# An encoder layer on one core: the Mamba-2 branch turned round, written in an order by hand for four engines, with weight fetches moved ahead

## The chip, the cores and the metric

The kernel runs on one core of a Trainium2 chip. The metric is the device time of one execution in microseconds (us). Five engines work beside each other: PE (TensorE, matmuls; its weight loads are shown as PEld), DVE (VectorE), ACT (ScalarE), POOL (GpSimd) and SP (SyncE, which here only issues DMAs). Each takes its instructions in a fixed order; where one waits, all behind it on that engine wait.

## The reference, cut to what matters

One layer: x is normalised and projected by one matrix `w_in` to the columns of three branches (Mamba-2, RWKV-7, HGRN2) and of three merge gates; each branch runs a scan forward and one backward and sums them; the branches are projected, gated, merged, and a feed-forward block follows. 1024 tokens, width 1024. The part that the change rewrites is the Mamba-2 branch (16 heads of 64, 2 groups of 8 heads, state 128, chunks of 128 tokens):

```python
xbc = jax.nn.silu(centred_depthwise_conv(xbc, conv_w, conv_b))
...
dt = jax.nn.softplus(dt_raw.reshape(b, L, 2, SSM_HEADS) + dt_bias)
y_f = ssd_chunked(xs, dt[:, :, 0], a[0], bm, cm)
y_b = flip_t(ssd_chunked(flip_t(xs), flip_t(dt[:, :, 1]), a[1], flip_t(bm), flip_t(cm)))
y = y_f + y_b + xs * d_skip[:, None]
y = y.reshape(b, L, SSM_INNER) * jax.nn.silu(z)
return rmsnorm(y, norm_w)
```

`ssd_chunked` computes in each chunk of 128 tokens: a part within the chunk (the products C·B, each times an exponential of differences of cumulated `dt*a`, applied to x), the chunk's own addition to the state (B times weighted x), and a part from the state that the chunk receives (C times that state, times an exponential).

## The kernel before

**The filler.** The input projection is cut into 79 jobs of 16 steps (`Jobs`, 1264 steps). A step is three matmuls of 128x512 (lines L330 to L332, `mm`): weights split in two parts `wh` and `wl`, x split likewise. The steps are handed out as filler between the pieces of the branches: `J.share(w)` emits a number of steps in proportion to `w` out of the table `FILL`, `J.get(...)` those that a branch needs first. Each job's 512 KB of raw weights come by a DMA that ACT issues (`wr`, L219), ACT casts them to `wh` (L221), DVE (or POOL) forms `wl` (L223). Results go from PSUM through `st` (L272) to DRAM (`pg` for the gates).

**The order.** A scheduler places instructions on each engine from the program's order, priorities and its own estimates of time, so that filler may be moved ahead of pieces that wait. Within `manual_schedule(engines=...)` the named engines keep the order in which the code is written.

**The Mamba-2 branch** (`ssd`, behind RWKV and HGRN2): a setup (`dt`, cumulated sums, their rows stored to DRAM as `cumd`), then for each of two groups: six convolutions (`conv`: tile `pt` from DRAM by SP, one ACT pass L1297, four DVE passes L1299, a Silu L1301), two for B and C and four for x; C·B products `cbps` (L1324), transposes `btps` (L1325) and `xps` (L1346, copied by ACT to `xt`); then the loop over i = 0..7, which I call the core: the forward chunk i and the backward chunk 7-i are treated in the same turn. `pairs` (L1362) makes the exponentials of a chunk for 8 heads: rows of `cumd` are broadcast by DMA into `E` (128x1024) for each direction, POOL subtracts (L1369), DVE picks one direction by a mask (L1372), ACT takes the exponential (L1373), DVE multiplies by C·B (L1374). PE computes `yo` (L1390, C times the state `S`), `st` (L1398, the chunk's addition to the state) and `yd` (L1409, eight products with `E`); DVE weights x (`xw`, L1396) and forms `yt` (L1392); POOL decays `S` (L1402) and adds to `Y` (L1393, L1383). `yo` and `st` share two PSUM buffers (tag `b`). In the region from L1378 only POOL's order is written by hand. After the core `Y` is transposed (`ytps`, L1429), multiplied by Silu(z) (`zs`) and stored.

## Time and profile before

| | before |
|---|---|
| median of 3 runs | 2424.53 us (2424.19 to 2427.28) |
| profiled execution | 2423.01 us, of which the trace spans 2421.3 us |
| mean granted TensorE clock | 0.973 |
| PE busy | 2272.7 us (94%) |
| DVE, POOL, ACT busy | 65%, 43%, 41% |
| first `st` of the core | at 1135.24 us of the span |

The span runs from the first instruction to the last. Busy shares overlap, since engines work beside each other; what an engine's idle time cost is read from its waits. Matmuls are pipelined: the durations of single matmuls overlap, so the time of one is read from the distance of two starts. An f32 matmul (`st`, `yo`, `yd`, the transposes) has two records each; an `mm` has one.

### The profile page before, as it was taken

The numbers are of one execution on the slowest core, as the hardware profiler recorded it, in microseconds if no ns is written. First come the engines' busy times: TensorE is split into PE (matmuls) and PEld (weight loads), VectorE is DVE, ScalarE is ACT, GpSimd is POOL, SyncE is SP. The second block draws the span as 40 slices with busy tenths as digits, with TensorE's granted clock in tenths as the row PEclk, the third lists the DMA queues.
The fourth block names the chain that finished last, engine by engine and source line by source line (L and its number), as shares of the span: only waits on it lengthen the run. The fifth ranks groups of instructions, "written<-read, shape, count | busy, mean of one in ns | idle before, by whom it ended". The sixth has DMA issues, their size and how long they took to land.

```text
span 2421.3 us, 37438 instructions
## 1 busy us (share of the span) xinstructions
PE 2272.7 (94%) x14785; PEld 1838.1 (76%) x14785; DVE 1570.6 (65%) x2041; ACT 988.7 (41%) x1436; POOL 1040.8 (43%) x817
## 2 busy tenths in 40 slices
PE   8998999999998998998999889999899999999895
PEld 6776778788777877887678567888688888877674
DVE  5678764455558568545856776442764554479999
ACT  6554532222466655435134154332433333344333
POOL 4433331543134335202941841430454444457985
PEclk9999999999999999999999999999999999999998
DMA  5455784764442232245545555541232222244211
GB/s 151 122 139 136 176 212 112 225 199 124 142 150 98 82 118 79 75 160 146 135 156 142 129 191 193 168 130 61 66 101 87 79 87 79 98 163 131 95 54 70
DMA packets 381212, 306.23 MB, mean 126 GB/s; under 512 B 111273, under 2 KB 323149, under 8 KB 381037
## 3 DMA queue, kind: packets, MB, share of 16 engines
q1 hardware_dynamic: 260909, 225.71, 31.7%
q10 hardware_dynamic: 119936, 77.61, 11.1%
q8 instruction: 116, 1.90, 0.3%
q0 software_dynamic: 192, 0.52, 0.1%
q14 instruction: 59, 0.48, 0.1%
HBM read 209.68 MB, written 94.11 MB: 125 GB/s over the span
## 4 chain that ended last, share of the span: by engine, by line
PE 61%; DVE 20%; POOL 5%; DMA 5%; issue 4%; ACT 4%; SPq 1%; ACTq 0%; DVEq 0%; POOLq 0%
PE mm L330 7%; PE mm L331 7%; PE mm L332 7%; PE ps L1588 6%; PE ps L1589 6%; PE ps L1590 6%; DVE ab L1805 3%; DVE acc L1927 2%; PE mm L231 2%; PE mm L232 2%; PE mm L233 2%; DMA E<-cumd 2%; POOL E L1369 2%; DVE rb L1805 1%; PE mm L1588 1%
## 5 line engine op out<-in xcount | busy, mean ns | idle before, releaser
L330 PE MATMUL mm<-x,wh 128*128 128x512 f32 (+1 forms) x1232 | 500.3, 406 | 0.6 <-ACT wh L221 0.5
L331 PE MATMUL mm<-x,wh 128*128 128x512 f32 (+1 forms) x1232 | 492.6, 400 | 0.0
L332 PE MATMUL mm<-x,wl 128*128 128x512 f32 (+1 forms) x1232 | 489.9, 398 | 0.0
L330 PEld LDWEIGHTS mm<-x,wh 128*128 128x128 f32 (+1 forms) x1232 | 232.8, 189 | 62.0 <-issue 10.3
L332 PEld LDWEIGHTS mm<-x,wl 128*128 128x128 f32 (+1 forms) x1232 | 232.8, 189 | 54.2 <-issue 4.6
L331 PEld LDWEIGHTS mm<-x,wh 128*128 128x128 f32 (+1 forms) x1232 | 232.8, 189 | 53.7 <-issue 7.0
L1589 PE MATMUL ps<-xb,rb 128*128 128x512 f32 x432 | 168.3, 390 | 0.0
L1590 PE MATMUL ps<-xb,rb 128*128 128x512 f32 x432 | 168.3, 390 | 0.0
L1588 PE MATMUL ps<-xb,rb 128*128 128x512 f32 x432 | 168.3, 390 | 0.0
L221 ACT CAST wh<-wr 128x1024 fp32r<-128x1024 f32 (+2 forms) x103 | 100.2, 973 | 109.4 <-PE mm L331 87.4
L1588 PE MATMUL ps<-rb,ab 128*128 128x512 f32 x308 | 125.9, 409 | 18.3 <-DVE acc L1927 17.4
L223 POOL TENSOR_TENSOR wl<-wr,wh 128x1024 fp32r<-128x1024 f32 x30 | 79.2, 2640 | 133.9 <-ACT wh L221 109.9
L1589 PE MATMUL ps<-rb,ab 128*128 128x512 f32 x308 | 123.7, 402 | 2.9 <-POOL rb L1805 2.9
L223 DVE TENSOR_TENSOR wl<-wr,wh 128x1024 fp32r<-128x1024 f32 (+2 forms) x73 | 95.2, 1303 | 44.9 <-ACT wh L221 44.8
L1590 PE MATMUL ps<-rb,ab 128*128 128x512 f32 x308 | 122.4, 400 | 1.5 <-DVE ab L1805 1.5
L1752 ACT CAST rb<-fs 128x512 fp32r<-128x512 f32 x85 | 52.6, 622 | 167.2 <-PE ps L1590 117.7
L272 ACT COPY st<-mm 128x512 f32<-128x512 f32 x130 | 75.3, 580 | 99.1 <-PE mm L332 82.9
L1369 POOL TENSOR_TENSOR E<-E,cums 128x1024 f32<-128x1024 f32 x32 | 69.3, 2178 | 65.5 <-DMA E<-cumd 45.3
L810 DVE TENSOR_TENSOR Gc<-Gps,mk 128x256 f32<-128x256 f32 x64 | 27.2, 425 | 106.0 <-PE Gps L807 59.9
L231 PE MATMUL mm<-oh,wh 128*128 128x512 f32 x224 | 89.5, 403 | 6.5 <-DVE gt L1492 4.3
L1927 DVE TENSOR_TENSOR acc<-acc,ps 128x512 f32<-128x512 f32 x148 | 94.1, 674 | 0.0
L1589 PEld LDWEIGHTS ps<-xb,rb 128*128 128x128 f32 x432 | 81.1, 188 | 16.9
(504 smaller groups left out, 5397.2 us busy)
## 6 DMA issues: line engine op xcount, KB each, us to landing
wr<-in_w_in_dram ACTq DMA_DIRECT2D x74, 512.0 KB
fr<-in_ffn_w_in_dram SPq DMA_DIRECT2D x44, 512.0 KB
E<-cumd SPq DMA_DIRECT2D x32, 512.0 KB
pg<-st ACTq DMA_DIRECT2D x48, 256.0 KB
gt<-pg SPq DMA_DIRECT2D x24, 512.0 KB
ad<-a SPq DMA_DIRECT2D x22, 512.0 KB
dr<-in_ffn_w_down_dram SPq DMA_DIRECT2D x22, 512.0 KB
ar<-ad SPq DMA_DIRECT2D x22, 512.0 KB
```

The costliest lines, as they stand in the source:

```text
L221: nc.scalar.copy(hi[:, :kt, :n], raw[:, :kt, :n])
L223: g.lo_eng.tensor_sub(lo[:, :kt, :n], raw[:, :kt, :n], f32(hi[:, :kt, :n]))
L231: nc.tensor.matmul(ps, whi[:, k, :n], xh, start=(k == 0), stop=False)
L330: g.nc.tensor.matmul(ps[:n], w[0][:, k, :n], xh, start=(k == 0), stop=False)
L331: g.nc.tensor.matmul(ps[:n], w[0][:, k, :n], xl, start=False, stop=False)
L332: g.nc.tensor.matmul(ps[:n], w[1][:, k, :n], xh, start=False, stop=(k == KT - 1))
L1369: nc.gpsimd.tensor_tensor(e, e, cs.unsqueeze(2).broadcast_to([P, 8, P]), SUB)
L1588: nc.tensor.matmul(ps, ah, bh, start=(i == 0), stop=False)
L1589: nc.tensor.matmul(ps, ah, bl, start=False, stop=False)
L1590: nc.tensor.matmul(ps, al, bh, start=False, stop=(i == n - 1))
L1805: eng.tensor_sub(blk[:, 1], s, f32(blk[:, 0]))
L1927: nc.vector.tensor_add(m[j], m[j], ps)
```

## The change

Three things, all inside one diff:

1. `Jobs` fetches the raw weights of job i+2 when the second half of job i begins (`fetch`), where before those of job i+1 were loaded when job i began.
2. The core is turned round. All seven states of the backward direction are formed first and kept (`Sb`), then one pass over the chunks i = 0..7 forms y of both directions, already transposed (channels on partitions): `yo` becomes four matmuls with a piece of the state as weights and `CT` as the moving side, for each direction, `yd` has `xt` (64 columns) as weights and `E` as the moving side and writes to alternating halves of the 128 partitions. The exponential of the row that `yo` is multiplied with (`X`) comes from the `E` tile by ACT. The transposes `ytps` after the core are gone. Silu(z) is computed before the core, stored to DRAM (`zd`) and read back chunk by chunk (`z`); the output goes out chunk by chunk. Of POOL's work, the decay of S goes to DVE, half of the subtractions to ACT (eight passes of 128x128 a chunk), the additions to `Y` fall away; a small one remains. DVE gets a second masked copy (`id8`), which sets the diagonal. `st` has PSUM tag `b` for itself; `yo` and `yd` share tag `a`.
3. The region written by hand now holds PE, ACT, DVE and POOL, and `FILL["ss"]` is a new table.

```diff
-    "ss": (4, 36, 12, 18, 6, 3, 8, 5, 22, 13, 8),
+    "ss": (4, 30, 12, 5, 5, 12, 22, 8, 5, 18),
...
+def load_raw(g, src, kt, n=P, tag="w"):
     raw = g.wpool.tile([P, KT, P], F32, tag=tag + "r", name=tag + "r", bufs=g.wraw_bufs)
     g.wq.dma_start(raw[:, :kt, :n], src.rearrange("(k p) c -> p k c", p=P))
+    return raw
+def load_w(g, src, kt, n=P, tag="w", raw=None):
+    nc = g.nc
+    if raw is None:
+        raw = load_raw(g, src, kt, n, tag)
...
+    def source(self, i):
+        job = self.jobs[i]
+        return self.g.A["w_in"][0][:, job.c0:job.c0 + job.n], KT, job.n
+    def fetch(self, i):
+        if 4 <= i < len(self.jobs) and i not in self.raws:
+            self.g.wq = self.g.nc.scalar
+            self.raws[i] = load_raw(self.g, *self.source(i))
...
+        return load_w(g, *self.source(i), raw=self.raws.pop(i, None))
...
         for half in range(2):
+            if half == 1:
+                self.fetch(i + 2)
...
-            nc.vector.tensor_sub(cums, cums, ld)
+            nc.vector.tensor_sub(cums, ld, cums)
...
+        m8, id8 = (kp.tile([P, P], U8, tag=n, name=n) for n in ("m8", "id8"))
         nc.vector.tensor_copy(m8, mlt)
+        nc.vector.tensor_copy(id8, g.ident)
...
-                J.share(F[1] + F[9] * grp)
+                J.share(F[1] + F[7] * grp)
...
+                nc.vector.tensor_add(gd, dtT[:, :, grp * 8:grp * 8 + 8], dtT[:, :, 16 + grp * 8:24 + grp * 8])
+                nc.vector.tensor_tensor(gd, gd, cbd.unsqueeze(2).broadcast_to([P, NT, 8]), MUL)
...
+                for q in range(grp * 4, grp * 4 + 4):
+                    zs = sp.tile([P, L + 4], F32, tag="E", name="zs", bufs=EB)[:, :L]
+                    nc.sync.dma_start(zs, J.get(g.pz, q))
+                    nc.scalar.activation(zs, zs, AF.Silu)
+                    nc.sync.dma_start(zd[q], zs)
...
+                def rows(c):
                     Es = []
                     for d in range(2):
                         e = sp.tile([P, L + 4], F32, tag="E", name="E", bufs=EB)
                         e = e[:, :L].rearrange("p (h t) -> p h t", t=P)
+                        h0 = d * 16 + grp * 8
+                        nc.sync.dma_start(e, cumd[h0:h0 + 8, c * P:(c + 1) * P].unsqueeze(0).broadcast_to([P, 8, P]))
                         Es.append(e)
+                    return Es
+                def exponents(c, Es):
+                    Xs = []
+                    for d in (1, 0):
+                        e, h0 = Es[d], d * 16 + grp * 8
+                        X = yp.tile([P, 4, P], F32, tag=f"X{d}", name="X", bufs=2)
+                        if c != (0, NT - 1)[d]:
+                            for b in range(2):
+                                hr = slice(b * 64, b * 64 + 64)
+                                nc.scalar.activation(X[hr], e[hr, b::2], AF.Exp)
+                        cs = cums[:, c, h0:h0 + 8]
+                        if d == 0:
+                            for h in range(8):
+                                nc.scalar.activation(e[:, h], e[:, h], AF.Identity, bias=cs[:, h:h + 1])
+                        else:
+                            nc.gpsimd.tensor_tensor(e, e, cs.unsqueeze(2).broadcast_to([P, 8, P]), ADD)
+                        Xs.insert(0, X)
+                    return Xs
+                def pick(Es):
+                    nc.vector.copy_predicated(Es[0], m8.unsqueeze(1).broadcast_to([P, 8, P]), Es[1])
+                def decays(c, e):
+                    nc.scalar.activation(e, e, AF.Exp)
+                    yield
+                    nc.vector.tensor_mul(e, e, CB[:, c:c + 1, :].broadcast_to([P, 8, P]))
+                    nc.vector.copy_predicated(e, id8.unsqueeze(1).broadcast_to([P, 8, P]),
+                                              gd[:, c].unsqueeze(2).broadcast_to([P, 8, P]))
+                    yield
+                def gate(c):
+                    z = yp.tile([P, 4, P], F32, tag="z", name="z", bufs=2)
+                    nc.sync.dma_start(z, zd[grp * 4:grp * 4 + 4, :, c * P:(c + 1) * P].rearrange("q p t -> p q t"))
+                    return z
...
+                Sb = yp.tile([P, NT - 1, 512], F32, tag="Sb", name="Sb")
+                Sa = yp.tile([P, 512], F32, tag="Sa", name="Sa")
+                def weighted(d, c):
+                    xw = yp.tile([P, 512], F32, tag="xw", name="xw", bufs=2)
+                    nc.vector.tensor_tensor(h3(xw), h3(xt[:, c]), per_head(wst, c, d), MUL)
+                    return xw
+                def update(d, c, xw, old, new):
+                    ps = pp.tile([P, 512], F32, tag="b", name="st", bufs=2)
+                    nc.tensor.matmul(ps, Bt[:, c], xw, start=True, stop=True)
+                    if old is None:
+                        nc.vector.tensor_copy(new, ps)
+                    else:
+                        nc.vector.tensor_tensor(h3(new), h3(old), per_head(dec, c, d), MUL)
+                        nc.vector.tensor_add(new, new, ps)
...
+                order = ExitStack()
+                order.enter_context(tc.manual_schedule(engines={PE, ACT, DVE, POOL}))
+                Es = rows(0)
+                X, z = exponents(0, Es), gate(0)
+                ahead = rows(1)
+                xw = weighted(1, NT - 1)
+                pick(Es)
+                for _ in decays(0, Es[0]):
+                    pass
+                J.share(F[9])
+                for c in range(NT - 1, 0, -1):
+                    xn = weighted(1, c - 1) if c > 1 else weighted(0, 0)
+                    update(1, c, xw, Sb[:, c] if c < NT - 1 else None, Sb[:, c - 1])
+                    xw = xn
+                    J.share(F[3])
+                for i in range(NT):
+                    ts = slice(i * P, (i + 1) * P)
+                    nEs = ahead
+                    if i + 2 < NT:
+                        ahead = rows(i + 2)
+                    if i + 1 < NT:
+                        nX, nz = exponents(i + 1, nEs), gate(i + 1)
+                    part = []
+                    for d, S in ((1, Sb[:, i] if i < NT - 1 else None), (0, Sa if i else None)):
+                        if S is None:
+                            continue
+                        ps = pp.tile([P, 4, P], F32, tag="a", name="yo", bufs=3)
+                        for q in range(4):
+                            nc.tensor.matmul(ps[:, q], S[:, q * P:(q + 1) * P], CT[:, ts], start=True, stop=True)
+                        nc.vector.tensor_mul(X[d], X[d], ps)
+                        part.append(X[d])
+                    if i < NT - 1:
+                        update(0, i, xw, Sa if i else None, Sa)
+                    J.share(F[4])
                     e = Es[0]
+                    ps = pp.tile([P, 4, P], F32, tag="a", name="yd", bufs=3)
                     for h in range(8):
+                        nc.tensor.matmul(ps[h % 2 * 64:h % 2 * 64 + 64, h // 2], xt[:, i, h * 64:h * 64 + 64], e[:, h],
                                          start=True, stop=True)
+                    y = part[0]
+                    if len(part) > 1:
+                        nc.vector.tensor_add(y, y, part[1])
+                    nc.vector.tensor_add(y, y, ps)
+                    nc.vector.tensor_mul(z, z, y)
+                    nc.sync.dma_start(ysc[grp * 4:grp * 4 + 4, :, ts].rearrange("q p t -> p q t"), z)
+                    nc.scalar.activation(y, z, AF.Square)
+                    nxt = iter(())
+                    if i + 1 < NT:
+                        pick(nEs)
+                        nxt = decays(i + 1, nEs[0])
+                        next(nxt)
+                    if i + 2 < NT:
+                        xw = weighted(0, i + 1)
+                    eng = nc.vector if grp and i == NT - 1 else nc.gpsimd
+                    eng.tensor_add(y[:, 0:2], y[:, 0:2], y[:, 2:4])
+                    if grp == 0:
+                        eng.tensor_add(ss[:, ts], y[:, 0], y[:, 1])
+                    else:
+                        eng.tensor_add(y[:, 0], y[:, 0], y[:, 1])
+                        eng.tensor_add(ss[:, ts], ss[:, ts], y[:, 0])
+                    next(nxt, None)
                     J.share(F[5])
+                    if i + 1 < NT:
+                        Es, X, z = nEs, nX, nz
```

What becomes of the order is seen at three places; the lines of the new code are about 20 higher in the parts before the core (L350 to L352 are the three matmuls of a filler step that were L330 to L332).

**PE, the setup of the first group, up to the first `st`.** Before (`btps` and `xps` are transposes of the setup, `mm` is filler):

```order
L332 MATMUL mm<-x_436,wl 128x512
L330 MATMUL mm<-x_190,wh 128x512
L1325 MATMUL btps<-ident,BT 128x128 x4
L1346 MATMUL xps<-ident,xq 128x128 x8
L331 MATMUL mm<-x_191,wh 128x512
L332 MATMUL mm<-x_190,wl 128x512
L330 MATMUL mm<-x_199,wh 128x512
L331 MATMUL mm<-x_200,wh 128x512
L332 MATMUL mm<-x_199,wl 128x512
L330 MATMUL mm<-x_208,wh 128x512
```

and now, at the corresponding place (the rows end with the first filler after the first `st`):

```order
L1345 MATMUL btps<-ident,BT 128x128
L1344 MATMUL cbps<-CT,BT 128x128
L1345 MATMUL btps<-ident,BT 128x128
L1344 MATMUL cbps<-CT,BT 128x128 x4
L1345 MATMUL btps<-ident,BT 128x128 x4
L1366 MATMUL xps<-ident,xq 128x128 x32
L1440 MATMUL st<-xw,Bt 128x512
L350 MATMUL mm<-x_199,wh 128x512
L351 MATMUL mm<-x_200,wh 128x512
```

Up to the end of the last but one run of `vps` matmuls (a product of HGRN2's last head) the filler is the same in both. Before, 12 steps follow and then the last 16 `vps`, and 127 more stand between these and the first `st`, so that 1026 of the 1264 steps are ahead of the first `st`. Now some 10 steps follow, then the last 16 `vps`, and no step stands between these and the first `st` (897 ahead of it); four stand between the first and the second `st`, and likewise behind each of the next. The filler that was among the end of HGRN2 and the setup has moved behind the first `st`.

**DVE, the start of the core.** Before:

```order
L223 TENSOR_TENSOR wl<-wr,wh 128x1024
L1396 TENSOR_TENSOR xw<-xt,wst 128x512
L1372 COPY_PREDICATED E<-m_10178,E 128x1024
L1396 TENSOR_TENSOR xw<-xt,wst 128x512
L1374 TENSOR_TENSOR E<-E,CB 128x1024
L223 TENSOR_TENSOR wl<-wr,wh 128x1024
L1372 COPY_PREDICATED E<-m_10178,E 128x1024
L1400 COPY S_10620<-st 128x512
L1396 TENSOR_TENSOR xw<-xt,wst 128x512
```

and now:

```order
L1319 SCALAR_TENSOR_TENSOR acc<-pt,vcolsv_443,acc 128x1024 x8
L1435 TENSOR_TENSOR xw<-xt,wst 128x512
L1413 COPY_PREDICATED E<-m_10174,E 128x1024
L1419 TENSOR_TENSOR E<-E,CB 128x1024
L1420 COPY_PREDICATED E<-id_10175,gd 128x1024
L230 TENSOR_TENSOR wl<-wr,wh 128x1024
L1435 TENSOR_TENSOR xw<-xt,wst 128x512
L1442 COPY Sb<-st 128x512
L1435 TENSOR_TENSOR xw<-xt,wst 128x512
```

The second `xw`, from which the second `st` is made, stood behind one mask copy of `E`; now it stands behind the whole chain of the first `E` (mask copy, product with C·B, diagonal) and behind a `wl` of the filler.

**ACT, the same place.** Before:

```order
L1347 COPY xt<-xps 128x4x128 x2
L1373 ACT_TABLE_LOAD
L1373 ACTIVATE E<-E 128x1024
L221 CAST wh<-wr 128x1024
L272 COPY st<-mm 128x512
L273 DMA pg<-st 128x512
L219 DMA wr<-in_w_in_dram 128x8x128
```

and now:

```order
L1401 ACT_TABLE_LOAD
L1401 ACTIVATE X<-E 64x512 x2
L1405 ACTIVATE E<-E,cums 128x128 x8
L1417 ACTIVATE E<-E 128x1024
L280 COPY st<-mm 128x512
L281 DMA pg<-st 128x512
L218 DMA wr<-in_w_in_dram 128x8x128
L280 COPY st<-mm 128x512
L281 DMA pg<-st 128x512
L228 CAST wh<-wr 128x1024
```

The DMA for `wr`, from which that `wl` comes, and the cast to `wh` stand behind the exponentials of the first chunk now; before, a `wr` and a cast stood directly beside them. One more difference lies far ahead of the Mamba-2 branch, on ACT in the first head pair of RWKV: the table that was loaded once (L376, before L221) is loaded earlier now, ahead of the tanh that replaces it, so that the chain of `E`, `kk`, `Em` loads its tables itself. Before and now:

```order
L413 ACTIVATE rx<-pt,mu_c_451 128x1024
L622 ACTIVATE E<-sg 128x8x64 x2
L219 DMA wr<-in_w_in_dram 128x8x128
L603 ACTIVATE kk<-kps,col 128x512
L623 ACTIVATE Em<-sg 128x512
L603 ACTIVATE kk<-kps,col 128x512
L623 ACTIVATE Em<-sg 128x512
```

```order
L433 ACTIVATE rx<-pt,mu_c_451 128x1024
L642 ACT_TABLE_LOAD
L642 ACTIVATE E<-sg 128x8x64 x2
L218 DMA wr<-in_w_in_dram 128x8x128
L623 ACT_TABLE_LOAD
L623 ACTIVATE kk<-kps,col 128x512
L643 ACT_TABLE_LOAD
L643 ACTIVATE Em<-sg 128x512
L623 ACT_TABLE_LOAD
L623 ACTIVATE kk<-kps,col 128x512
L643 ACT_TABLE_LOAD
```

Five loads of a table stand there that did not before.

84 lines of the change are left out of this document (6 added, 78 removed).

## The prediction

> **What bounds the kernel now.** I read the page from the top (busy shares, chain), then the windows around the Mamba-2 branch, the waits of PE there, and the timeline.
>
> ```profile
> span 2421.3 us, 37438 instructions
> ...
> PE 2272.7 (94%) x14785; PEld 1838.1 (76%) x14785; DVE 1570.6 (65%) x2041; ACT 988.7 (41%) x1436; POOL 1040.8 (43%) x817
> ...
> PE 61%; DVE 20%; POOL 5%; DMA 5%; issue 4%; ACT 4%; SPq 1%; ACTq 0%; DVEq 0%; POOLq 0%
> ```
>
> PE is busy for 94% of the span and carries 61% of the chain that ended last. Filler steps can be moved, but not dropped: a microsecond in which PE stands idle is won or lost for good. So I keep an account of PE's idle time. The windows (length, then busy time of PE, PEld, DVE, ACT, POOL, then granted clock, DMA share, GB/s) are the end of HGRN2 with the setup of group 0, the core of group 0, the setup of group 1, the core of group 1:
>
> ```profile
> 1027.00:1135.20 108.20, 108.20 (x583) 90.75 (x582) 54.20 (x58) 54.06 (x76) 8.04 (x18) 1.00 0.50 142
> 1135.20:1253.00 117.80, 105.97 (x463) 78.20 (x463) 78.29 (x75) 29.29 (x34) 80.98 (x48) 0.94 0.52 138
> 1253.00:1333.00 80.00, 80.00 (x390) 66.61 (x388) 48.92 (x43) 36.76 (x48) 15.28 (x19) 1.00 0.61 170
> 1333.00:1460.00 127.00, 107.44 (x452) 77.35 (x452) 95.09 (x95) 42.75 (x48) 80.16 (x49) 0.93 0.60 169
> ```
>
> In the setup PE never stands (108.20 of 108.20, 80.00 of 80.00). In the cores it stands 11.8 + 19.6 = 31.4, and runs at a mean clock of 0.94 and 0.93, which costs another 0.06 x 106.0 + 0.07 x 107.4 = 13.9: 45 us are lost there. PE's waits say to whom (us in total, times, longest):
>
> ```profile
> PE yd L1409 <- DVE E L1374: 7.6, 3, 6.4
> PE yo L1390 <- DVE S L1400: 7.5, 1, 7.5
> PE st L1398 <- DVE S L1403: 6.5, 10, 1.4
> PE yo L1390 <- DVE yt L1392: 3.5, 3, 1.7
> ```
>
> Behind these DVE products stands POOL (81 of 117.8 us busy): decay, sums and subtractions. That is the loss which the change attacks.
>
> **The hole that the new order makes.** The first term is the order of PE. Up to the last `vps` the filler is the same in both; then 127 steps stood ahead of the first `st` and now none. The price of a step is the distance of two like matmuls:
>
> ```profile
> 1028.80 1.15 PE L1053 MATMUL vps<-lv 128*64 128x64 f32 x32
> ...
> 1133.65 0.39 PE L332 MATMUL mm<-x,wl 128*128 128x512 f32 x1
> ...
> 1134.33 0.39 PE L332 MATMUL mm<-x,wl 128*128 128x512 f32 x1
> ...
> 1135.24 1.02 PE L1398 MATMUL st<-xw,Bt 128*128 128x512 f32 x2
> ```
>
> 1134.33 - 1133.65 = 0.68 us. So of the 108.2 us from 1027 to the first `st`, 129 x 0.68 = 88 are filler, and 20 are PE's small pieces of the setup. In the new order PE has only those 20 us to do until the setup has run through: how long that takes decides the result. The chain it has to run:
>
> ```profile
> 1060.36 0.69 DVE L1197 TENSOR_TENSOR t<-t 128x512 f32<-128x512 f32 x1 [2.72 <-ACT t L1196]
> ...
> 1063.61 0.20 POOL L1283 MEMSET mlt<- 128x128 f32 x1 [29.72 <-DMA out_h<-t]
> ...
> 1070.09 1.23 ACT L1297 ACTIVATE acc<-pt,vcolsv 128x1024 f32<-128x1024 f32 x1
> ...
> 1082.31 7.38 DVE L1299 SCALAR_TENSOR_TENSOR acc<-pt,vcolsv,acc 128x1024 f32<-128x1024 f32 x6
> ...
> 1097.05 1.06 ACT L1301 ACTIVATE BT<-acc 128x1024 f32<-128x1024 f32 x1
> ...
> 1130.53 0.69 DVE L1396 TENSOR_TENSOR xw<-xt,wst 128x512 f32<-128x512 f32 x1 [6.14 <-ACT xt L1347]
> ```
>
> (a) The end of HGRN2: from 1028.80 to the start of the branch at 1063.61, 34.8 us, in which PE's small pieces stood behind filler. Without it I estimate 20 to 21, so the branch starts near 1048 instead of 1063.6. (b) Six convolutions, which share five buffers and so hardly overlap: each one ACT pass of 1.23, four DVE passes of 7.38/6 = 1.23, one Silu of 1.06, 7.2 in all, 43 for six; the first starts 6.5 after the branch does (1070.09 - 1063.61); waits for the tile's DMA and for the buffers between them I put at 8 to 10, which gives the first `xw` 58 after the start (before it took 66.9). So the first `st` comes at about 1107. (c) Four filler steps follow, and then PE waits for the second `xw`, which DVE has behind the first `E` with all its chain. That chain starts at SP's DMA queue: four `zs` loads, one `E`, four `zd` stores and only then the second `E`, which also needs a buffer that a `zs` held. How long an `E` takes to land:
>
> ```profile
> 1115.50 11.43 SPq L1366 DMA_DIRECT2D E<-cumd  x4
> ...
> 1124.07 2.08 POOL L1369 TENSOR_TENSOR E<-E,cums 128x1024 f32<-128x1024 f32 x1 [14.12 <-DMA E<-cumd]
> 1131.32 1.90 POOL L1369 TENSOR_TENSOR E<-E,cums 128x1024 f32<-128x1024 f32 x1 [5.17 <-DMA E<-cumd]
> ```
>
> The first landed 8.6 us after it was issued (1124.07 - 1115.50), the next 7.2 later. After the last convolution's tiles come free (start + 57) I count 7 for the last `zs`, 1 for its Silu, 8.6 for the store's issue and the second `E`: start + 73. Then the table load, the two `X` passes and eight short ACT passes, mask copy, exponential: 7; the `wr` DMA that ACT issues only now, its landing, cast, `wl` and `xw`: 8. That is start + 88, or 1136. At 1136 the kernel before had done 126 more steps than the new one will have: 126 x 0.68 = **86 us** of PE time to make up. Bounds: if (c) hides behind (b) and the second `st` comes with the first, at 1107, it is 57; if every step of (c) is as slow as its slowest row, at 1152, it is 102. I take 86, since the order on SP, ACT and DVE puts these steps one behind the other.
>
> **The clock.** After long idle PE is slow at first:
>
> ```profile
> 1140.00:1150.00 10.00, 2.46 (x16) 1.99 (x16) 3.57 (x4) 1.06 (x1) 5.50 (x4) 0.79 0.74 222
> 1150.00:1160.00 10.00, 8.27 (x32) 5.44 (x31) 10.00 (x8) 1.53 (x2) 9.56 (x5) 0.84 0.59 107
> ```
>
> One idle stretch of some 7.5 us costs 0.21 x 2.5 + 0.16 x 8.3 = 1.8 us of work afterwards. I add **2** for the end of the hole; inside it PE mostly waits, so that slow small pieces cost only where they stand in the chain. The Trainium skill ("TensorE: Matmul & The Clock Gate", "What's actually happening") says that PE falls to half clock after one idle window of about 3.4 us and rises after a busy one. By this rule, the sum would be up to 10 us higher, an estimate, since most of the hole's 20 us of small pieces would run at half speed; no row shows small pieces after so long a hole.
>
> **The core, turned round.** What a turn costs PE now: 14 filler steps x 0.68 = 9.5, two `yo` and a `st` at about 0.9 each (the row of `st` has 1.02 for its two records, which overlap what follows), `yd` 1.1 to 1.9: 13.3 to 14.1. DVE per turn: two masked copies, the product with C·B, one `xw`, seven half-size passes (0.69 each, as `t` above) and most of a `wl` (1). POOL keeps one subtraction and small sums; what it did beside goes to DVE and ACT or falls away, so PE no longer waits for it.
>
> ```profile
> L1372 DVE COPY_PREDICATED E<-m,E 128x1024 f32<-128x1024 uint8 x16 | 35.0, 2187 | 39.3 <-POOL E L1369 39.3
> L1374 DVE TENSOR_TENSOR E<-E,CB 128x1024 f32<-128x1024 f32 x16 | 26.4, 1650 | 2.8 <-ACT E L1373 2.8
> L1396 DVE TENSOR_TENSOR xw<-xt,wst 128x512 f32<-128x512 f32 x28 | 37.7, 1349 | 6.1 <-ACT xt L1347 6.1
> ```
>
> With these means (2.19, 1.65, 1.35, taken beside a busy POOL) DVE needs 2 x 2.19 + 1.65 + 1.35 + 7 x 0.69 + 1 = 13.2 a turn, less beside an idle POOL. So PE bounds the turn by a little. DMA is as near: 0.52 of 117.8 over eight turns is 7.7 us of the sixteen queues a turn; the third more filler adds 1, and reading `z` and writing the output in pieces of 512 bytes adds two transfers of 1024 packets. Their price from the queue of `E` (packets, MB, share of 16 engines; 1160 to 1240):
>
> ```profile
> q1 hardware_dynamic: 8801, 6.24, 32.2%
> ```
>
> 0.322 x 80 x 16 / 8801 = 47 ns a packet, 3.0 us a transfer: 7.7 + 1 + 6 = 14.7 at this price, 12.2 at half of it. The Trainium skill ("DMA: Bandwidth & Descriptors", "Specifications") has pieces from 512 bytes on at line rate; by that a transfer would take some 1.5 us (an estimate) and the sum be 7 us lower. The trace doesn't bear it out for `E`.
>
> I expect that of the 45 us lost in the cores 17 stay (the first turns of each group, the new setup of group 1, some turns bound by DMA or DVE): **-28**. Bounds: all 45 gone; nothing gained.
>
> **PE work that falls away or gets dearer.**
>
> ```profile
> 446.25 1.15 PE L838 MATMUL Sps<-UV,Btc 128*64 128x64 f32 x32
> ...
> 1139.74 1.89 PE L1409 MATMUL yd<-xt,E 128*128 128x64 f32 x16
> ...
> 1256.45 1.03 PE L1429 MATMUL ytps<-ident,Y 128*128 128x128 f32 x8
> ```
>
> The 64 transposes `ytps` at 1.03/8 = 0.13 or a little less: **-7**. `yd`: 128 products at 1.89/8 = 0.24. The new form has 64 columns of weights and alternates between the halves of the partitions, as `Sps` does, where 16 products took 1.15, 0.07 each with half the moving columns; so 0.14 for the new `yd`: 128 x 0.10 = **-12**. Bounds: 0 (no overlap of the halves) and -14. The Trainium skill ("TensorE: Matmul & The Clock Gate", "Part 3: Packing small matmuls — row/col tiling") says that a weight load overlaps running matmuls only if the row group differs, which it does not here; by that the gain would be near 0 and the sum 12 higher. `Sps` shows such an overlap all the same: 0.07 each. `yo` in four pieces with 128 moving columns is as much work as before: 0.
>
> **The table loads in RWKV** (five more on ACT in the first head pair):
>
> ```profile
> L376 ACT ACT_TABLE_LOAD x8 | 10.3, 1283 | 0.1
> ...
> PE Aps L653 <- DVE BK L634: 12.6, 2, 7.8
> ```
>
> 5 x 1.28 = 6.4 us in the chain of `E`, `kk` and `Em`, at whose end PE waits for `BK` as it is: **+6**. Bounds: 0 (filler covers it) and 12 (another cold clock).
>
> **The raw weights one and a half jobs ahead**: 0. PE's wait for `wh` is 0.6 us on the whole kernel:
>
> ```profile
> L330 PE MATMUL mm<-x,wh 128*128 128x512 f32 (+1 forms) x1232 | 500.3, 406 | 0.6 <-ACT wh L221 0.5
> ```
>
> The weights are there already; before the Mamba-2 branch ACT issues `wr` at the same places in both orders. Bounds: -0.6 and, where the DMA stands behind an exponential, what (c) counts already. The bank of its own for `st`: PE waited for a bank's reader (`yt`) 3.5, within the 45.
>
> **The sum**: +86 + 2 - 28 - 7 - 12 + 6 = +47, on the profiled execution's 2423.0: 2470. It stands 1.5 below the median of the runs, so that 2471 is the time to compare with 2424.5. A difference under 0.2%, 4.8 us, could not be told from none.
>
> **Rivals.** (1) Faster: DVE starts the six convolutions back to back and the `zs` loads hide. Without the hole the sum is -39; it turns at a hole of 39 us, that is with the second `st` at 1136 - 47 = 1089, 41 after the branch's start, less than the 43 of the convolutions' own passes. It needs overlap between them, which the 54.20 us of DVE in 108.2 allow. With the second `st` at 1083 the hole is 33 and the time 2418. (2) DMA or DVE bound the turns: at 15.5 us a turn instead of 13.9, 16 turns lose 26 more: 2497. For it: 13.2 and 14.7 above. Against it: POOL's share falls, and with it DVE's durations. (3) PE's small pieces run cold in the hole and no `yd` halves overlap: 10 + 12, 2493. (4) The reordering does nothing: the engines' real waits would have to hold PE before as well; the row 108.20 of 108.20 speaks against that.
>
> **Chances.** My forecast (a hole of 57 to 102, turns bound by PE) 0.57, (1) 0.13, a hole that just balances 0.06, (2) 0.16, (3) 0.08. So faster 0.13, same 0.06, slower 0.81. The forecast's own range is 2440 to 2490; with half of (2) and (3), and the smaller hole towards (1), 2428 to 2505.
>
> **What would show it.** Right: PE idle for some 60 us or more between HGRN2's last products and the second `st`, with `xw` waiting for DVE or the DMA of `E`; no `ytps`; turns of 14 us with PE at 1.00; `yd` at 0.14. Wrong: the second `st` before 1090, or idle PE in the turns behind DVE's `E` or the DMA of `z`.

## The result: 101 us slower, and the profile after

| | before | after |
|---|---|---|
| median, all runs of that comparison | 2424.36 us (2422.8 to 2427.28) | 2524.98 us (2517.45 to 2531.8) |
| ratio of the times | | 1.0414, 95% interval [1.0397, 1.043] |
| profiled execution, its span | 2423.01, 2421.3 us | 2517.45, 2515.7 us |
| mean granted TensorE clock | 0.973 | 0.954 |

Slower, as forecast, but by twice as much: 2471 was predicted, at most 2505. The profiled execution of the changed kernel is the fastest of its four, so the comparison of the two traces explains 94 of the 101 us. From the page:

```profile
span 2515.7 us, 37916 instructions
...
PE 2266.2 (90%) x14889; PEld 1838.5 (73%) x14889; DVE 1587.2 (63%) x2097; ACT 1066.4 (42%) x1628; POOL 932.1 (37%) x765
...
PE 61%; DVE 20%; DMA 7%; issue 5%; ACT 4%; POOL 2%; SPq 1%; ACTq 0%; DVEq 0%; POOLq 0%
```

PE is busy 6.5 us less (2266.2 against 2272.7) in a span 94.4 us longer: all of the loss is idle PE, 249.5 us instead of 148.6. POOL has 109 us less to do, which did not make up for it. The windows of the changed kernel show where PE stands: from the end of HGRN2 to the second `st`, the core of group 0, a part of the setup of group 1, the end of that setup with the start of its core, and its turns.

```profile
1035.00:1163.00 128.00, 36.86 (x209) 29.99 (x210) 48.63 (x55) 45.16 (x66) 6.06 (x17) 0.64 0.41 117
1163.00:1300.00 137.00, 130.61 (x676) 102.70 (x676) 105.87 (x116) 72.36 (x131) 30.70 (x31) 0.96 0.53 141
1300.00:1330.00 30.00, 30.00 (x146) 25.25 (x145) 17.12 (x17) 13.58 (x17) 0.26 (x4) 1.00 0.51 157
1330.00:1400.00 70.00, 52.64 (x221) 41.07 (x220) 19.70 (x23) 22.98 (x37) 1.90 (x1) 0.85 0.59 165
1400.00:1500.00 100.00, 100.00 (x549) 79.30 (x548) 79.12 (x87) 57.98 (x114) 34.51 (x26) 1.00 0.65 156
```

91 us of idle PE lie in one hole of 128 us, 17 more in the start of group 1's core. In the regular turns PE doesn't stand; the 6.4 us of the second window lie ahead of the last `yd` of group 0. What PE waited for between 1020 and 1500 (total, times, longest):

```profile
PE st L1440 <- DVE xw L1435: 56.8, 4, 37.5
PE xps L1366 <- ACT xq L1321: 20.3, 3, 7.5
PE dtps L1267 <- DMA ot<-out_r: 14.2, 1, 14.2
PE cbps L1344 <- ACT CT L1321: 7.2, 1, 7.2
PE yd L1484 <- DVE E L1420: 6.4, 1, 6.4
```

The two largest waits stand ahead of the second `st` of each group, 37.5 and 14.1 us. `xps`, `dtps` and `cbps` belong to the setup, which filler covered before; the wait of `yd` is that of the last turn of group 0. The timeline of PE there, with one batch of small pieces in the hole, the start of `yo` in two turns that follow each other, and the setup and second `st` of group 1:

```profile
1034.92 1.15 PE L1073 MATMUL vps<-lv 128*64 128x64 f32 x32
...
1106.44 1.97 PE L1366 MATMUL xps<-ident,xq 128*128 128x128 f32 x8 [7.46 <-ACT xq L1321]
...
1119.81 2.08 PE L1440 MATMUL st<-xw,Bt 128*128 128x512 f32 x2 [1.98 <-DVE xw L1435]
...
1162.63 2.07 PE L1440 MATMUL st<-xw,Bt 128*128 128x512 f32 x2 [37.46 <-DVE xw L1435]
1168.55 1.02 PE L1440 MATMUL st<-xw,Bt 128*128 128x512 f32 x2
...
1191.27 1.09 PE L1484 MATMUL yd<-E,xt 128*64 128x128 f32 x16
...
1212.71 1.05 PE L1475 MATMUL yo<-CT,Sb 128*128 128x128 f32 x8
...
1226.17 1.05 PE L1475 MATMUL yo<-CT,Sb 128*128 128x128 f32 x8
...
1338.08 1.04 PE L1366 MATMUL xps<-ident,xq 128*128 128x128 f32 x8
...
1386.94 2.08 PE L1440 MATMUL st<-xw,Bt 128*128 128x512 f32 x2 [14.11 <-DVE xw L1435]
```

The hole reaches from 1036 to 1162.6, where 1027 to 1136 was predicted. A transpose leaves one record, not two (`xps` has 64 on the page for its 64), so a row of `xps` x8 is eight transposes. The chain of work that ended last has in it, between the two `st`:

```profile
1118.59 9.36 DMA zd<-zs
1128.01 11.31 DMA E<-cumd
1139.34 0.63 ACT X L1401
...
1146.48 13.18 DMA wr<-in_w_in_dram
...
1160.75 1.23 DVE wl L230
1161.98 0.61 DVE xw L1435
1162.63 2.07 PE st L1440 x2
```

Three DMAs one behind the other take 34 of the 44 us: the store of `zd`, whose landing frees a buffer; the second `E`, which SP issues as soon as that store has landed (1118.59 + 9.36 = 1127.95); and the filler's raw weights, which ACT issues only after the exponentials.

### The profile page after: what moved, and what is told of

Same layout as the page of the kernel before. It is cut to its first block, busy times and chain, and to the rows that moved or that the text cites. A ratio compares the mean times of both kernels' runs of the same rounds, so it can differ in the third digit from the quotient of the medians.

```text
span 2515.7 us, 37916 instructions
## 1 busy us (share of the span) xinstructions
PE 2266.2 (90%) x14889; PEld 1838.5 (73%) x14889; DVE 1587.2 (63%) x2097; ACT 1066.4 (42%) x1628; POOL 932.1 (37%) x765
## 4 chain that ended last, share of the span: by engine, by line
PE 61%; DVE 20%; DMA 7%; issue 5%; ACT 4%; POOL 2%; SPq 1%; ACTq 0%; DVEq 0%; POOLq 0%
PE mm L350 7%; PE mm L352 7%; PE mm L351 6%; PE ps L1664 6%; PE ps L1665 6%; PE ps L1666 6%; PE mm L238 2%; PE mm L239 2%; PE mm L240 2%; DVE ab L1881 2%; DMA wr<-in_w_in_dram 2%; DVE acc L1319 2%; DVE acc L2003 2%; PE Gps L827 1%; PE mm L1664 1%
## 5 line engine op out<-in xcount | busy, mean ns | idle before, releaser
L350 PE MATMUL mm<-x,wh 128*128 128x512 f32 (+1 forms) x1232 | 509.0, 413 | 0.6 <-ACT wh L228 0.5
L352 PE MATMUL mm<-x,wl 128*128 128x512 f32 (+1 forms) x1232 | 487.6, 396 | 0.0
L350 PEld LDWEIGHTS mm<-x,wh 128*128 128x128 f32 (+1 forms) x1232 | 234.1, 190 | 66.5 <-issue 14.8
L352 PEld LDWEIGHTS mm<-x,wl 128*128 128x128 f32 (+1 forms) x1232 | 233.3, 189 | 52.1 <-DVE wl L230 0.5
L1407 POOL TENSOR_TENSOR E<-E,cums 128x1024 f32<-128x1024 f32 x16 | 33.8, 2114 | 203.6 <-ACT X L1401 196.0
```

The costliest lines, as they stand in the source:

```text
L350: g.nc.tensor.matmul(ps[:n], w[0][:, k, :n], xh, start=(k == 0), stop=False)
L352: g.nc.tensor.matmul(ps[:n], w[1][:, k, :n], xh, start=False, stop=(k == KT - 1))
```

## The experiments

Sixteen kernels were run, each compared with the kernel before on the same chip; the medians of before were 2422.8 to 2424.4. The expectations number their theories: 1, the hole comes from PE's order by hand, which holds the region's filler behind the first `st`; 2, the wait between the first and the second `st` comes from the chain of the first `E`; 3, the early fetch is worth nothing and costs its table loads; 3b, in an order by hand the landing of `wr` is a wait that the distance of the fetch sets.

| kernel | its base and edit | median us | ratio to before, 95% interval |
|---|---|---|---|
| b_pe | before, PE by hand | 2471.2 | 1.0203 [1.018, 1.0227] |
| b_pef2 | b_pe, filler given to the setup | 2453.7 | 1.0115 [1.0096, 1.0135] |
| b_fetch | before, early fetch | 2431.9 | 1.0033 [1.0022, 1.0045] |
| a_poolonly | after, only POOL by hand | 2458.7 | 1.0152 [1.0131, 1.0172] |
| a_late2 | after, first chunk's exponentials later | 2486.6 | 1.0264 [1.0245, 1.0283] |
| a_nofetch | after without the early fetch | 2596.4 | 1.072 [1.0696, 1.0744] |
| a_f8 | after, fetch from the ninth job | 2513.6 | 1.0379 [1.0358, 1.04] |
| a_fetch0 | after, fetch two jobs ahead | 2478.6 | 1.0231 [1.0209, 1.0253] |
| a_bank | after, yo in the tag of st | 2524.3 | 1.0428 [1.0404, 1.0452] |
| l_fill_f8 | a_late2 with a_f8, filler to the setup | 2478.4 | 1.023 [1.0215, 1.0245] |
| n_z | a_late2 with a_f8, zs in its own tile | 2469.2 | 1.0189 [1.0163, 1.0214] |
| n_d | n_z, filler to the setup | 2440.2 | 1.0063 [1.0041, 1.0084] |
| n_e2 | n_d, fetch two jobs ahead | 2430.4 | 1.0032 [1.0021, 1.0044] |
| n_f2 | n_e2, filler to group 1's setup | 2452.6 | 1.0127 [1.011, 1.0145] |
| n_h | n_e2, xw earlier on DVE | 2432.2 | 1.0041 [1.0026, 1.0057] |
| n_h2 | n_h, another FILL | 2435.1 | 1.0052 [1.0039, 1.0065] |

**b_pe: the old core with PE's order by hand.**

```diff
-                order.enter_context(tc.manual_schedule(engines={POOL}))
+                order.enter_context(tc.manual_schedule(engines={PE, POOL}))
```

> The kernel before with one word more: PE's order in the region of the core is written by hand too (the core itself is the old one). In its order 905 filler steps stand ahead of the first st instead of 1026, and none between the last vps and the first st but 6. Theory 1 (the hole comes from PE's order by hand, which keeps the region's filler behind the first st): PE idles 60 to 80 us before the first st, as in the changed kernel up to its first st at 1119.8, and the time is 2424 + 55 to 85, about 2495. Rival (the hole comes from the new core's own start: zs, zd, E, X): PE idle before the first st under 15 us, time within 20 us of 2424.

One word costs 47 us (2471.2). The first `st` comes at 1111.6 and PE has, from the last `vps` up to it:

```profile
1030.00:1112.00 82.00, 35.08 (x216) 28.83 (x216) 43.64 (x49) 34.70 (x50) 5.97 (x17) 0.68 0.34 100
```

47 us idle and the rest at a clock of 0.68: the hole, with the old core and without `zs`, `zd` or `X`. The rival falls. The hole comes from the order by hand, which holds the region's filler behind the first `st`. But the time is under my range (2479 to 2509) and the idle time under the 60 to 80 us that I expected. The filler that is kept back also helps the old core: its two groups leave PE idle for 10.2 us (1112 to 1235) and 10.1 us (1310 to 1440), where before it was 11.8 and 19.6.

**a_poolonly: the new core without the order by hand.** The reverse edit on the changed kernel.

> The changed kernel with only POOL's order written by hand, as before the change; everything else of the change stays. In its order 1027 filler steps stand ahead of the first st, as in the kernel before. Theory 1: PE doesn't stand in the setup, the first st comes at 1140 to 1150, and the gains of the new core show: -7 (transposes), -13 (yd), and some of the 45 us lost in the old cores, against +6 (table loads) and the end of group 1, where filler has run out: 2405 to 2435. Rival (the turned core itself is what costs, through DMA or DVE): above 2470.

2458.7: the hole is gone (between 1027 and the first `st` at 1148 PE waits for 0.8 us; 1027 steps stand ahead of it), and 66 us of the loss with it. But it stays 36 us slower than before, above the range: the table loads are in it, and in the scheduler's order the new core makes PE wait.

```profile
PE yd L1484 <- DVE E L1420: 24.7, 5, 11.4
PE st L1440 <- DVE Sa L1445: 18.1, 2, 14.6
```

Theory 1 holds for the hole. The gains of the new core that I expected behind it did not show.

**a_late2: the first chunk's exponentials behind the fourth backward state.**

```diff
-                X, z = exponents(0, Es), gate(0)
                 ahead = rows(1)
                 xw = weighted(1, NT - 1)
-                pick(Es)
-                for _ in decays(0, Es[0]):
-                    pass
                 J.share(F[9])
...
                     xw = xn
+                    if c == 4:
+                        X, z = exponents(0, Es), gate(0)
+                        pick(Es)
+                        for _ in decays(0, Es[0]):
+                            pass
                     J.share(F[3])
```

> The changed kernel with the exponentials of the first chunk (X, the eight ACT passes, POOL's addition, mask copy, exponential, product, diagonal) moved from ahead of the backward states to behind the fourth of them; nothing else. PE's order is the same. Theory 2 (42.8 us between the first and the second st, 37.5 of them idle, come from the chain of the first E ahead of the second xw, and 19.6 us with 14.1 idle in group 1): the second st follows within 10 us of the first, at 1120 to 1130, and the time falls by 35 to 50, to about 2480. Rival (what PE waits for is the wr DMA and the wl of the filler, which come late anyway): the second st stays later than 1150 and the time falls by under 10.

2486.6, 38 less than the changed kernel, and the second `st` follows after 5.3 instead of 42.8 us:

```profile
1123.95 2.07 PE L1440 MATMUL st<-xw,Bt 128*128 128x512 f32 x2 [1.98 <-DVE xw L1435]
1129.27 1.02 PE L1440 MATMUL st<-xw,Bt 128*128 128x512 f32 x2
```

As expected: theory 2 holds. Some of the wait moved to a later `st` (26.7 us in five waits are left).

**a_nofetch: without the early fetch.**

```diff
-        if 4 <= i < len(self.jobs) and i not in self.raws:
+        if False and 4 <= i < len(self.jobs) and i not in self.raws:
```

> The changed kernel without the early fetch: the raw weights are loaded when the job before begins, as in the kernel before. In its order the five table loads of RWKV's first head pair are gone (6 loads ahead of that place instead of 12), so it is the fetch that moved them. Theory 3: the fetch itself is worth nothing and the table loads cost what PE's longer wait for vx shows (8.1 instead of 1.7 us): 6 us faster than the changed kernel. Rival (the fetch helps in the core, where filler and wr meet): 5 us or more slower than the changed kernel.

2596.4, 71 us slower than the changed kernel. Theory 3 falls; the rival (5 us or more slower) holds, with a size that I had not thought of. What ACT waited for, first here (1160 to 1330), then in the changed kernel (1160 to 1320):

```profile
ACT wh L228 <- DMA wr<-in_w_in_dram: 65.2, 7, 13.2
```

```profile
ACT wh L228 <- DMA wr<-in_w_in_dram: 27.1, 6, 11.7
```

ACT waits up to 13.2 us for raw weights beside the core's other DMAs, and a job's 16 steps alone take 16 x 0.68 = 10.9. In the order by hand the cast on ACT and `wl` on DVE stand at a fixed place, so that a late landing stops the exponentials, `xw` and the outputs behind them too. PE's wait for `xw` is 79.1 us in all, against 56.8 in the changed kernel, and it waits 28.5 for `wh`. The fetch is what makes the order by hand bearable; a_fetch0 below shows that one and a half jobs ahead are still not enough.

**b_fetch: the early fetch alone, in the kernel before** (the diff's parts in `Jobs` and `load_w`, nothing of `ssd`).

> The kernel before with the early fetch alone. The order on PE is the same as before; on ACT the five table loads of RWKV's first head pair appear. Theory 3 (where the scheduler places the filler, the fetch is worth nothing, and it costs its table loads): 6 us slower than before, 3 to 11. Rival (the fetch is worth as much here as in the order by hand, where taking it out cost 71 us): 10 us or more faster.

8 us slower (0.33%), inside the range of theory 3. Where the scheduler places the filler, the fetch and its table loads together gain nothing; no run has the fetch without the loads there. In RWKV's first pair PE waits (before, then b_fetch)

```profile
PE vps L674 <- DVE vx L415: 1.7, 1, 1.7
```

```profile
PE vps L693 <- DVE vx L434: 8.1, 1, 8.1
```

The profiled execution of b_fetch is its fastest (2425.3), so its trace shows the 6.4 us at this place and only 2.3 at the end of the span.

**a_f8: the early fetch from the ninth job on.**

```diff
-        if 4 <= i < len(self.jobs) and i not in self.raws:
+        if 8 <= i < len(self.jobs) and i not in self.raws:
```

> The changed kernel with the early fetch from the ninth job on only; the first head pair of RWKV then has its tables as in the kernel before (6 loads there instead of 12), and the region of the core keeps the fetch. Theory: the table loads cost what PE waits longer for vx, 6 us: 2519 against 2525, and the last vps of HGRN2 comes some 6 us earlier than at 1034.9. Rival (what is late in RWKV is caught up by filler before HGRN2 ends): no difference, last vps within 2 us.

2513.6, 11 us less than the changed kernel, by the medians of four runs each, whose ranges overlap; the two traces differ by 6.6. The last `vps` of HGRN2 starts at 1029.9 instead of 1034.9, and PE's wait for `vx` is 1.7 us again. The table loads of RWKV come from the fetch of the jobs 5 to 8, and their price is passed on to the end.

**a_bank: yo in the tag of st again.**

```diff
-                        ps = pp.tile([P, 4, P], F32, tag="a", name="yo", bufs=3)
+                        ps = pp.tile([P, 4, P], F32, tag="b", name="yo", bufs=2)
```

> The changed kernel with yo in the PSUM tag of st again (two buffers for both, as before the change), yd alone in the other. Theory (the bank apart is worth little, since DVE empties yo within a microsecond): 0 to 10 us slower than the changed kernel. Rival (it is what lets st run ahead of yo in a fixed order): 25 us or more slower, with PE waiting for X or S in each turn.

2524.3, the same as the changed kernel. One new wait is to be seen (`st` for the reader of `yo`, 10.4 us in four), and the sum doesn't move. A bank of its own for `st` is worth nothing that these runs can tell.

**l_fill_f8: filler put back in the hole.** a_late2, the fetch of a_f8, and

```diff
-    "ss": (4, 30, 12, 5, 5, 12, 22, 8, 5, 18),
+    "ss": (4, 30, 12, 5, 5, 12, 177, 8, 5, 18),
```

> Three edits together: the exponentials of the first chunk behind the fourth backward state, the early fetch from the ninth job on, and a table FILL in which the setup of the first group gets 177 instead of 22, so that 79 more filler steps stand ahead of the first st (976) and 11 instead of 14 in a turn. Theory 1: the hole of 85 us with 20 us of work that was left shrinks by 79 x 0.68 = 54, less some 9 by which the filler delays the setup; with 6 for the table loads 2486.6 - 54 + 9 - 6 = 2436, 2425 to 2445. Rival (turns of 11 steps fall under what DVE needs, so that the filler is missed there): 2455 or more, with PE waiting for DVE in the turns.

2478.4, 8 us less than a_late2, which the table loads alone explain. The rival holds by its time and in part by its cause: PE waited 43.0 us for `xw`, in eight places, of which four in the turns make 13, while the two largest (12.4 and 10.1) still stand ahead of a backward `st` of each group. The setup, behind filler again, ran longer (first `st` at 1129.95 instead of 1123.95, although the table loads are gone), and the chain of `zs`, `zd` and `E` came later with it. Filling the hole pays only when the chain behind it doesn't hang on the same late point.

**b_pef2: b_pe with 290 instead of 22 for the setup in FILL.**

> The kernel before with PE's order written by hand (as in b_pe, 48 us slower than before) and in FILL 290 instead of 22 for the setup, so that 1023 filler steps stand ahead of the first st, 20 of them between the last transposes, and 5 to 9 fewer in a turn of the core. Theory 1 (what made b_pe slower is filler that is missing in the setup, not the order by hand as such): the idle time before the first st goes from 60 to under 10 us and the time to 2471 - 50 + 10 = 2431, 2415 to 2440. Rival (the old core needs the filler where the scheduler had it): PE idles in the core instead, 2455 or more.

2453.7: 18 us less than b_pe, not 40, and between the two ranges. The setup is full, and the old core is not (first from 1027 to 1135, then the core of group 0):

```profile
1027.00:1135.00 108.00, 108.00 (x581) 90.31 (x580) 54.33 (x58) 55.23 (x77) 6.90 (x18) 1.00 0.47 138
1135.00:1250.00 115.00, 86.83 (x357) 59.84 (x356) 68.63 (x67) 24.24 (x27) 81.54 (x48) 0.91 0.49 127
```

The hole is closed by filler alone, which is theory 1; the 28 us of idle PE in the core of group 0, where b_pe had 10, are the rival's. The filler is a fixed sum of 1264 steps: what the setup gets, the core lacks, unless its chain is shorter than PE's work.

**n_z: zs in halves of 512 columns in the tile of z.** a_late2, the fetch of a_f8, and

```diff
-                    zs = sp.tile([P, L + 4], F32, tag="E", name="zs", bufs=EB)[:, :L]
-                    nc.sync.dma_start(zs, J.get(g.pz, q))
-                    nc.scalar.activation(zs, zs, AF.Silu)
-                    nc.sync.dma_start(zd[q], zs)
+                    for h in range(2):
+                        zs = yp.tile([P, 512], F32, tag="z", name="zs", bufs=2)
+                        nc.sync.dma_start(zs, J.get(g.pz, q)[:, hs(h)])
+                        nc.scalar.activation(zs, zs, AF.Silu)
+                        nc.sync.dma_start(zd[q][:, hs(h)], zs)
```

> The changed kernel with three edits: the exponentials of the first chunk behind the fourth backward state, the early fetch from the ninth job on, and zs in halves of 512 columns in a tile of its own (that of z), so that Silu(z) is computed and stored during the setup and the first E's need not wait for the buffers that zs held. The filler stays as in the changed kernel (897 steps ahead of the first st). Theory 2: the rest of the chain of zs, zd and E goes, that is 26.7 us in which st waited for xw and 8.4 in which yd waited for E in the kernel with the first edit alone (2486.6), and 8 for the table loads: 2448, 2440 to 2460. Rival (the DMAs of E, z and wr are late for other reasons): above 2470.

2469.2: PE's wait for `xw` falls from 26.7 to 9.2 us, and the time by 17, of which 8 to 11 are the table loads. About half of what was expected; neither range holds it.

**n_d: n_z with 280 instead of 22 for the setup in FILL.**

> As n_z, and in FILL 280 instead of 22 for the setup: 1011 filler steps ahead of the first st, spread over the setup as in the kernel before, and 10 instead of 14 in a turn. Both theories together: no hole of 60 us ahead of the first st, 12 at most; turns that DVE bounds with about 11.5 us instead of PE's 13.5: 2448 - 55 + 10 + 16 = 2419, 2405 to 2435; it would beat both kernels. Rival (with less filler the turns are bound by the DMAs of E, z and wr at about 13 us): 2440 or more, PE waiting for E, xw or S in each turn.

2440.2, 29 us less than n_z: above the theory's range, at the rival's bound. The hole is closed, and the turns of group 0 are not full (first the end of HGRN2 with the setup, then the turns):

```profile
1027.00:1140.00 113.00, 106.59 (x558) 87.31 (x557) 56.55 (x64) 60.89 (x84) 4.13 (x16) 0.97 0.58 177
1170.00:1280.00 110.00, 98.52 (x528) 78.00 (x526) 88.22 (x91) 63.55 (x113) 26.09 (x31) 0.92 0.68 173
```

In the chain of work between 1190 and 1260 the landing of `wr` stands for 36%; one of its pieces:

```profile
1201.91 12.25 DMA wr<-in_w_in_dram
```

**a_fetch0: the fetch two jobs ahead, in the changed kernel.**

```diff
-            if half == 1:
+            if half == 0:
                 self.fetch(i + 2)
```

> The changed kernel with the raw weights fetched when the first half of the job before the last begins (fetch at half 0 instead of half 1: two jobs ahead instead of one and a half). On ACT the wr DMA whose landing took 13.2 us between the first and the second st then stands ahead of the exponentials of the first chunk; RWKV's first pair has 6 table loads instead of 12. Theory 3b (in an order by hand the landing of wr is a wait that the distance of the fetch sets): the second st comes 13 us earlier, 10 in group 1, with 8 to 11 for the table loads 2525 - 32 = 2493, 2485 to 2505; DVE's wait for wh in the region falls under 5 us. Rival (the wait is for E and zd alone): as a_f8, 2514.

2478.6: 46 us less than the changed kernel, more than expected (the traces differ by 37: 2479.2 against 2515.7 of span, the changed kernel's being its fastest). Not all of it is the distance: the table loads of RWKV's first pair are gone here too (last `vps` at 1028.60 instead of 1034.92), so that a_f8, which has them gone as well, is the kernel to compare with, and 35 us are left. The second `st` comes 29.7 us after the first instead of 42.8, and in group 1 7.3 instead of 19.6:

```profile
1143.09 2.07 PE L1440 MATMUL st<-xw,Bt 128*128 128x512 f32 x2 [24.31 <-DVE xw L1435]
```

So 13 and 12 us were the landing of `wr`, as theory 3b has it. DVE's wait for `wh` between 1100 and 1500 falls from 69.6 to 47.2 us, and not under 5, as I had expected.

**n_e2: n_d with the fetch two jobs ahead** (the same edit).

> As n_d (2440.2), with the raw weights fetched two jobs ahead. In n_d the turns with 10 steps take 11 to 16 us instead of the 10.6 that PE needs, and the chain of waits shows the landing of wr (12 to 13 us) in them. Theory 3b: 16 turns lose 1 to 1.5 us less each, and the starts of both cores some 5: 2440 - 22 = 2418, 2408 to 2428, faster than the kernel before. Rival (DVE with 11 us a turn, or the DMAs of E and z, hold the turns): within 5 us of 2440.

2430.4, 10 us less than n_d: theory 3b by its direction, at less than half its size; neither range holds it, and it is still 7 us slower than before.

**n_f2: n_e2 with 45 instead of 8 for the setup of group 1.**

> As n_e2, with 11 steps fewer ahead of the first st and some 25 more in the setup of group 1 (FILL 45 instead of 8 for it), where n_d left PE idle for 14.5 us of 70. Theory (the filler is a fixed sum; what counts is that no stage lacks it): n_e2 less 5 to 10 us. Rival (what is given there is missing in the first setup and the turns): the same as n_e2 within 3 us.

2452.6, 22 us slower than n_e2: against both expectations. The window from 1027 to 1140 in n_e2, then in n_f2:

```profile
1027.00:1140.00 113.00, 106.70 (x554) 87.62 (x553) 56.41 (x62) 61.33 (x86) 4.13 (x16) 0.95 0.58 179
```

```profile
1027.00:1140.00 113.00, 99.05 (x519) 81.07 (x518) 55.29 (x61) 60.06 (x84) 4.13 (x16) 0.91 0.57 172
```

With 11 steps fewer ahead of the first `st` PE stands 7.6 us longer there. The setup of group 1 (1280 to 1350) did gain 6.1 us of idle time by its filler, but the first states and turns of group 0 (1140 to 1280) lost 7.4 and the end (1460 to 1540) 8.5. That is the rival's cause, at a size it did not have.

**n_h: xw made earlier on DVE; n_h2: with another FILL.**

```diff
                         update(0, i, xw, Sa if i else None, Sa)
+                    if i + 2 < NT:
+                        xw = weighted(0, i + 1)
                     J.share(F[4])
...
-                    if i + 2 < NT:
-                        xw = weighted(0, i + 1)
```

> As n_e2 (2430.4), with the weighted x (xw) of the next chunk made right behind the state's update instead of behind the output's sums, the mask copy and the exponential. In n_e2 PE waits 23.1 us for xw, nine times. Theory 2 (what stands ahead on DVE in the fixed order is the wait): most of it goes, 2430 - 15 = 2415, 2408 to 2422, faster than the kernel before. Rival (xw was only the first of several that come late; yo, yd or E take its place): 2426 to 2432.

> As n_h with another FILL: 9 more filler steps ahead of the first st (1020), 8 instead of 9 or 10 in a turn, and more in the setup of group 1. Theory (the filler is a fixed sum, and turns short of it are bound by DVE): within 10 us of n_h, on either side; slower if the turns fall under DVE's need.

2432.2 and 2435.1: no gain. In n_h the wait for `xw` falls from 23.1 to 12.4 us, and those for `E` and `X` take its place (n_e2's row, then n_h's):

```profile
PE st L1441 <- DVE xw L1436: 23.1, 9, 5.9
```

```profile
PE st L1441 <- DVE xw L1436: 12.4, 4, 4.5
PE yd L1488 <- DVE E L1421: 8.6, 3, 4.3
...
PE yd L1488 <- ACT X L1402: 3.7, 2, 1.9
```

n_h lies just above its rival's range (2426 to 2432), n_h2 within the 10 us of n_h that were expected. No version beat the kernel before; the best, n_e2, is 0.3% slower.

## Why the prediction was right and wrong, step by step

The traces give the account. From the start of the last `vps` to the first product of the merge behind the branch (1034.92 to 1517.9 now, 1028.80 to 1430.7 before, with 2.6 us added for 20 `ytps` that came later) the time is 483.0 instead of 404.5 us: some 78 more. 6 lie ahead of it and 10 behind. The prediction had 41 in the branch, 6 ahead and 0 behind. Of the 38 or so that it missed in the branch, half are the hole (105 for 86) and half the other terms together (core, transposes, `yd`, clock: -26 where -45 was forecast). The 10 behind are a term that I put at nothing: at the start of the merge PE waits 7.5 us for DVE's `m`, before 1.5.

- **The hole** (+86): right in cause, shown by b_pe with the old core and by a_poolonly with the new one, and too small. PE's work of 23 us (20 of small pieces, 3 of filler, at full speed) stood in 127.7 us (1034.9 to 1162.6), 105 lost instead of 86, and above my bound of 102. (a) The branch started at 1057.7 instead of 1048; 6 of that are the table loads. (b) From there to the first `xw` it took 61.4 us, 58 expected: nearly right. (c) is the step that failed: 43 us from the first `st` to the second, 29 expected. I allowed 14.6 from the first `st` to the landing of the second `E`, and it took 19.5: the store of `zd` and this `E` were counted at 8.6 together, where they took 9.4 and 11.3 one behind the other, since SP issued the `E` only when the store had landed. And I allowed 8 for `wr` with cast, `wl` and `xw`, which took 16.1, the landing alone 13.2. a_late2 and a_fetch0 show both.
- **The clock** (+2): too small, and the first half of rival (3) had the mechanism. The granted clock over the hole is 0.64, and three of the four `xps` batches of group 0 have 1.97 us for eight transposes that take 1.04 in the setup of group 1. Here the trace agrees with what the Trainium skill has on the clock gate in "TensorE: Matmul & The Clock Gate", "What's actually happening": after idle windows these pieces ran at half speed. At 0.64 the 36.9 us in which PE was busy in the hole hold 0.36 x 36.9 = 13 us of slowness, an estimate; how much of that stood in the chain no run separates.
- **The core** (-28): wrong, and with the hole the second step that failed. The regular turns came as worked out: 13.46 us (1212.71 to 1226.17), 13.3 to 14.1 predicted, and over the six from 1199.2 to 1280.0 PE is busy for 80.80 of 80.80 us at a clock of 1.00. So rival (2) falls:

```profile
1212.70:1226.20 13.50, 13.50 (x78) 10.85 (x77) 12.46 (x13) 8.92 (x19) 3.75 (x3) 1.00 0.72 197
```

DVE is busy for 12.5 us of a turn, its mask copy at 1.32 us instead of 2.19, beside a POOL that is busy for 3.75 of the 13.5 us instead of 81 of 117.8. The DMA engines are busy for 0.72 x 13.5 = 9.7, where 14.7 was added up: `z` and the output are 256 KB each, 512 pieces, and not the 1024 of the prediction (whose sum at half the price would be 11.7, not 12.2). But 37 us are lost in the cores all the same: 6.4 + 0.04 x 130.6 to 1300, 17.4 + 0.15 x 52.6 to 1400. Against the 45 before that is -8. The 17 I left for "first turns and setup" missed that group 1 begins with the same chain of `zd`, `E` and `wr` as group 0, with 14.1 us of waiting.
- **The transposes and yd** (-7, -12): right. `yd` takes 1.09/8 = 0.136 a product, 0.14 predicted. What I drew from the rule of the Trainium skill on weight loads ("TensorE: Matmul & The Clock Gate", "Part 3: Packing small matmuls — row/col tiling"), a gain near 0, did not come. With the same 128 moving columns a `yo` product, which has 128 columns of weights, takes 1.05/4 = 0.26, twice as long as a `yd`: the two halves overlap.
- **The table loads** (+6): right in size. PE waits 8.1 instead of 1.7 us for `vx`, and the last `vps` comes 6.1 us later; b_fetch is 8 slower, and a_f8 gave 11 back.
- **The raw weights** (0): a term put at nothing for a wrong reason. I read the wait of PE for `wh`, 0.6 us in the kernel before, as the worth of the fetch. In that kernel the scheduler could move casts and filler to where the weights had landed, which is my explanation and not shown by a run of its own. In the order by hand the fetch is worth 71 us, with its table loads already paid (a_nofetch), and half a job more another 35 (a_fetch0 against a_f8). What its distance cost in the hole sat in my sum in (c), as a landing of `wr` that I had put too short. That the table loads are caused by the fetch I had not seen either.
- **A bank of its own for `st`** (0): right, by a_bank.
- **Rival (1)**, faster by a short hole, was wrong, and its premise, that without the hole the new core is 39 us ahead, showed in no run: with the hole closed, the chain moved and the fetch at two jobs (n_e2) the time is 2430. Why isn't settled. What the runs show is that filler taken for the setup is missed in the turns (b_pef2, n_d), and that each wait taken away there lets another one come up (n_h).

## What to carry to other kernels

Before an engine's order is fixed by hand, ask what the scheduler had carried across the border of that region: filler emitted inside it can't be moved ahead any more, and the stage before it stands bare (b_pe: one word, 47 us). A fixed order also turns every landing into a wait of all that stands behind it, so the distance of a fetch that was worth nothing can become the largest term; price it by the landing time inside the stage, not by the wait of a kernel in which the order could give way. And filler is a fixed sum: what one stage is given, another lacks (b_pef2: the setup full, the core 28 us idle).

## What the runs showed of the hardware that was not expected

A DMA of 512 KB landed 9.4 (`zd`), 11.3 (`E`) and 13.2 us (`wr`) after its issue at the start of the core, where the first `E` of the kernel before took 8.6. And small pieces between waits ran at half speed: the first two `st` 2.07 and 2.08 instead of 1.02, and the three batches of eight `xps` that stood behind waits of 5.4 to 7.5 us 1.97 instead of 1.04. It was not so throughout: the first batch of `xps`, right behind the C·B products, took 1.09, and the mean granted clock of the hole is 0.64.
